# Halving the last RWKV norm, starting the output projection with the second half of the tokens, and moving the norms' low parts to VectorE

## The chip, the cores and the metric

The kernel runs on one core of one Trainium2 chip. The metric is the device time of one execution in microseconds, the median of several runs. A core has TensorE (PE, matmuls; weight loads are PEld), VectorE (DVE), ScalarE (ACT), GpSimd (POOL) and SyncE (SP, which issues most of the transfers). All five run their own instruction streams in order and wait for one another by semaphores. TensorE's clock has two levels, 1.2 and 2.4 GHz; a granted clock of 1.00 in the profile is the upper one, 0.50 the lower.

## What is computed

Two layers of a bidirectional encoder on 1024 tokens of width 1024, in float32. A layer is

```
h = rms_norm(x); proj = h @ w_in            # retention, RWKV-7, differential attention
y = concat(retention, rwkv7, attention)     # 8 blocks of 128 features: 0-2, 3-5, 6-7
x = x + y @ w_out                           # output projection
h = rms_norm(x); x = x + (silu(h @ w_gate) * (h @ w_up)) @ w_down
```

RWKV's result is normalised per head, gets a bonus, and is multiplied by a gate (`(norm(y) + bonus) * gate`) before it goes into `y`. Only that last step of RWKV (`rwkv_fin`), the projection with `w_out` and the RMS norms matter here.

## The kernel before

Activations lie with features on the 128 partitions and tokens in the free dimension. A tensor of 1024 x 1024 is 8 feature blocks k, each cut into two halves of 512 tokens; nearly every instruction works on a 128 x 512 tile. A dense product is made exact by splitting both factors into a high part and a low part (`split`: ACT writes the high part `hi`, then DVE or POOL subtracts it from the source to give `lo`), and by three matmuls hi*hi, hi*lo, lo*hi for each k (`dense`: 24 matmuls for 8 k). Tiles are called hh/hl (activations), sh/sl (activations of the Strassen-like sums) and whh/wll (weights); `wr` is a raw weight tile as loaded.

**The mixer's second part** (`rwkv`) interleaves, by a hand-written order on PE, ACT, DVE and POOL, the RWKV recurrence (`rwkv_rec`: one `U`, one `S` on ACT and a few small matmuls for every step, in windows w), the preparation of later windows, the retention (`ret_pair`, tile `rt` in its head norm) and, for each of three head pairs p, the last step `rwkv_fin`. In that order a list `beside` holds generators; every entry has a rate, and a `yield` is a place where other work is put in between. `rwkv_fin(p)` runs in the first window after pair p is complete, on both halves of the tokens at once; for the last pair it stands after everything else. Its head norm (`head_norm`, tile `fq`) is Square on ACT, a matmul `vps`, Ln on ACT, Exp on ACT, a product on DVE, a scale on ACT; Ln and Exp each load a function table. Then come the bonus (`bo`, loaded), the gate matmul `gps` (its operand `gl` is loaded), two DVE operations and a store to `mixed[3 + p]` in DRAM (`mix`). The recurrence runs through the tokens in both directions, so the second half of y is complete one window before the first half. Four buffers, a ring, are shared by y, bo, gl and the bonus's tiles; the later memory pools (H for hh/hl, W for weights) lie on the mixer's memory and a tile in them waits for the old tiles it overlaps.

**The output projection** (`phase_c`, `out_blocks`) loads the 16 half blocks of `mixed` (tile `mixl`, line 1421), first half first, splits them, loads all 16 tiles of x (line 1560), and then loads the w_out blocks (line 222). SP issues all of these, in the order in which a planner puts them out at compile time; the order follows the program text and modelled times. The first four output blocks cb are computed for half 0 and half 1 in turn, then cb 4 to 7 for half 0, then for half 1.

**The FFN's start** (`phase_c` after `out_blocks`) is the RMS norm of both halves (norm_sq, norm_rs with the matmul `nps` and the tile `nrs`, norm_out on line 262), and the operands of a Strassen-like scheme: B11, B21 from half 0, B22 from half 1, and the sums T1 to T4 (`ops_sums`), each with a split. About half of the low parts are made on POOL (`eng=gp` or `g`). The weights of the first gate and up blocks (q == 0) are split in 7 pieces each (`set_split`), low parts on POOL. `norm_split` at the start of a layer does the same with 16 tiles, low parts of odd k on POOL.

Of the kernel before, what the change touches and what calls it, by code (L numbers as in the profile page):

```python
# [17 lines left out]
T = 1024  # L18
# [159 lines left out]
class Net:  # L178
# [48 lines left out]

    def dense(self, ps, w, acts):

        n = len(acts)  # L230
        for k, (ah, al) in enumerate(acts):
            hi, lo = w[k]
            self.mm(ps, hi, ah, start=k == 0, stop=False)
            self.mm(ps, hi, al, start=False, stop=False)
            self.mm(ps, lo, ah, start=False, stop=k == n - 1)
# [572 lines left out]
    def head_norm(self, y, eps, w, b, q):  # L808

        nc = self.nc  # L810
        ps = []
        for half in range(2):
            self.act(q[:, half * 512:half * 512 + 512], y[half], AF.Square)
        yield 2
        for half in range(2):
            ps.append(self.bank([128, 512], "vps"))
            self.mm(ps[half], self.bones, q[:, half * 512:half * 512 + 512])
        yield
        for half in range(2):
            self.act(q[:, half * 512:half * 512 + 512], ps[half], AF.Ln, scale=1.0 / 64, bias=eps[:, 0:1])  # L820
            self.free(ps[half])
        self.act(q, q, AF.Exp, scale=-0.5)
        yield
        for half in range(2):
            sl = slice(half * 512, half * 512 + 512)
            self.tt(q[:, sl], y[half], q[:, sl], ALU.mult)
            self.act(q[:, sl], q[:, sl], AF.Identity, scale=w, bias=b)

    def rwkv_fin(self, l, st):
        nc = self.nc  # L830
        p = st["p"]
        pp = self.par[l][:, P_PAIR + p * PP:P_PAIR + (p + 1) * PP]
        yield
# [5 lines left out]
        for half in range(2):  # L839
            sl = slice(half * 512, half * 512 + 512)  # L840
# [5 lines left out]
        for half in range(2):  # L846
            sl = slice(half * 512, half * 512 + 512)
            t = q[:, sl]
            yield 1
            ps = self.bank([128, 512], "gps")  # L850
            self.mm(ps, lg, gl[half])
            self.tt(t, t, bo[half], ALU.add)
            yield
            self.tt(t, t, ps, ALU.mult)
            self.free(ps)
            nc.sync.dma_start(out=self.mixed[3 + p][:, sl], in_=t)

    def rwkv(self, l):
# [35 lines left out]
        for w in range(-2, 12):  # L894
# [57 lines left out]
        run(ret[0], self.rwkv_fin(l, sts[2]))  # L952
# [344 lines left out]
    def op(self, ops, name, t, eng=None):  # L1297
        p, tag = (self.S, "s") if name in ("T2", "T3", "T4") else (self.H, "h")
        ops[name].append(self.split(p, t, (tag, tag), eng=eng))

    def ops_sums(self, ops, bs, names=("T1", "T2", "T3", "T4")):

        g = self.nc.gpsimd
        for n in names:
            for i, (b11, b12, b21, b22) in enumerate(bs):
                e = g if i % 2 else None
                if n == "T1":
                    self.tt(b12, b12, b11, ALU.subtract)
                    self.op(ops, n, b12, g)
                elif n == "T2":  # L1310
                    self.tt(b22, b22, b12, ALU.subtract)
                    self.op(ops, n, b22, e)
                elif n == "T3":
                    self.tt(b11, b22, b11, ALU.subtract)
                    self.op(ops, n, b11, g)
                else:
                    self.tt(b21, b21, b22, ALU.subtract)
                    self.op(ops, n, b21, e)

    def set_load(self, src):  # L1320
# [7 lines left out]
        return dict(A11=a[:, :4], A12=a[:, 4:], A21=b[:, :4], A22=b[:, 4:], w={})  # L1328
# [38 lines left out]
    def out_blocks(self, l, x, acts):  # L1367

        order = [(cb, half) for cb in range(4) for half in range(2)]
        order += [(cb, half) for half in range(2) for cb in range(4, 8)]  # L1370
        w = {}
        for cb, half in order:
            if cb not in w:
                w[cb] = self.weights(self.ia["w_out"][l, cb])
            ps = self.psd.tile([128, 512], F32, tag="d", name="aps")
            self.dense(ps, w[cb], acts[half])
            self.tt(x[half][cb], ps, x[half][cb], ALU.add)
# [37 lines left out]
    def phase_c(self, l):  # L1415
        nc = self.nc
        acts = [[], []]
        for half in range(2):
            for k in range(8):
                m = self.S.tile([128, 512], F32, tag="s", name="mixl")  # L1420
                nc.sync.dma_start(out=m, in_=self.mixed[k][:, half * 512:half * 512 + 512])
                acts[half].append(self.split(self.H, m, ("h", "h")))
        x = self.load_x(self.xs)
        self.out_blocks(l, x, acts)
# [5 lines left out]
        gp = nc.gpsimd  # L1430
        with self.tc.high_priority(offset=100000):
# [6 lines left out]
            for k in range(8):  # L1438
                self.op(ops, "B21" if k >= 4 else "B11", self.norm_out(n[0], g, k, x[0], x[0][k]),
                        gp if k % 2 else None)  # L1440
            self.norm_sq(n[1], x[1], range(4, 8))
            self.norm_rs(n[1])
            for k in (4, 5, 6, 7, 0, 1, 2, 3):
                t = self.norm_out(n[1], g, k, x[1], x[1][k])
                if k >= 4:
                    self.op(ops, "B22", t, gp if k % 2 else None)
# [18 lines left out]
        return self.down(l, hid, xm)  # L1465
# [22 lines left out]
    def down(self, l, hid, xm):  # L1488
# [4 lines left out]
        for cb0 in (0, 4):  # L1493
            accs = []
            for half in range(2):
# [145 lines left out]
```

## Time and profile before

| | |
|---|---|
| time, median of 3 runs | 3538.19 us (3536.35 to 3542.45) |
| time of the profiled execution | 3539.07 us |
| its span, first to last instruction | 3537.3 us |
| PE busy | 3213.3 us (91%) |
| DVE, ACT, POOL busy | 2002.5, 1555.9, 941.8 us |
| mean granted TensorE clock | 0.951 |

The span is cut into stages. In layer 0 the mixer's second part ends near 940 us, the output projection runs from 976 to 1068 us, the FFN's first products from 1076 us on, and layer 1 begins near 1760 us; layer 1 repeats the pattern some 1747 us later. A busy time is read against its own stage: PE's 91% of the whole hides stretches in which it stands still.

### The profile page before, as it was taken

Reading aid. Unit: us, or ns where it says so; the run is one execution under the profiler, and the core shown is the slowest. Engines: PE = TensorE matmul, PEld = TensorE weight load, DVE = VectorE, ACT = ScalarE, POOL = GpSimd, SP = SyncE. Lnnn points to the kernel's source line nnn. Section 1 sums busy time; section 2 is a strip of 40 time slices with the busy share of each in tenths; the row PEclk is TensorE's granted clock in tenths of the full one; section 3 lists DMA queues with packets and bytes.
Section 4 is the critical chain, followed back from the end, with each engine's and each line's share of the span. In section 5 each row is a group of like instructions: output and inputs, shape, how many; then the busy total and the mean of one; then the engine's idle time right before and its main releaser. Section 6 shows DMA issues by size and latency. Waiting matters only on the chain.

```text
span 3537.3 us, 71264 instructions
## 1 busy us (share of the span) xinstructions
PE 3213.3 (91%) x29148; PEld 2595.5 (73%) x29148; DVE 2002.5 (57%) x3725; ACT 1555.9 (44%) x2975; POOL 941.8 (27%) x800
## 2 busy tenths in 40 slices
PE   6999799998697999999979997998986989999997
PEld 4778587777475888888867776877874768888886
DVE  4798526676338555552338975176662485555433
ACT  4566444656424333342236664356554333332322
POOL 3222220000036545422132221200001365544220
PEclk9999799999798999999999998999987999999998
DMA  5544324433431222283044533244425112223721
GB/s 172 153 144 121 116 104 156 137 118 107 144 105 60 84 75 92 78 286 119 27 159 129 153 110 124 98 155 141 138 75 188 72 51 93 78 78 117 264 72 48
DMA packets 214063, 419.02 MB, mean 118 GB/s; under 512 B 23876, under 2 KB 58948, under 8 KB 213700
## 3 DMA queue, kind: packets, MB, share of 16 engines
q1 hardware_dynamic: 191000, 378.53, 32.5%
q0 software_dynamic: 10064, 12.85, 1.7%
q10 hardware_dynamic: 12672, 23.07, 1.7%
q8 instruction: 230, 3.77, 0.5%
q14 instruction: 97, 0.79, 0.1%
HBM read 313.67 MB, written 100.70 MB: 117 GB/s over the span
## 4 chain that ended last, share of the span: by engine, by line
PE 72%; DVE 11%; DMA 6%; ACT 5%; issue 2%; POOL 2%; SPq 0%; DVEq 0%; ACTq 0%; POOLq 0%
PE sp L194 22%; PE dn L194 13%; PE dps L194 13%; PE aps L194 4%; DMA wr<-in_w_in_dram 2%; PE ns L194 2%; PE y L194 2%; DVE pt L1217 1%; PE pv L194 1%; PE tps L1247 1%; POOL wll L188 1%; ACT L185 1%; DVE x L188 1%; PE s L194 1%; PE yps L194 1%
## 5 line engine op out<-in xcount | busy, mean ns | idle before, releaser
L188 POOL TENSOR_TENSOR wll<-wr,whh 128x512 fp32r<-128x512 f32 x416 | 556.8, 1341 | 1576.6 <-ACT whh L185 1554.7
L185 ACT ACTIVATE whh<-wr 128x512 fp32r<-128x512 f32 x416 | 260.7, 630 | 627.2 <-PE sp L194 165.8
L194 PE MATMUL dps<-hl,whh 128*128 128x512 f32 x960 | 383.3, 399 | 6.7 <-POOL hl L188 3.5
L194 PE MATMUL dps<-hh,whh 128*128 128x512 f32 x960 | 386.9, 403 | 0.9 <-DVE stl L377 0.8
L194 PE MATMUL dps<-hh,wll 128*128 128x512 f32 x960 | 382.7, 399 | 1.2 <-POOL wll L188 1.2
L194 PE MATMUL sp<-hh,whh 128*128 128x512 f32 x704 | 278.2, 395 | 8.8 <-ACT hh L185 8.8
L194 PE MATMUL sp<-hl,whh 128*128 128x512 f32 x704 | 281.4, 400 | 2.8 <-POOL hl L188 2.5
L194 PE MATMUL sp<-hh,wll 128*128 128x512 f32 x704 | 276.4, 393 | 0.3 <-POOL wll L188 0.3
L194 PE MATMUL dn<-hh,whh 128*128 128x512 f32 x704 | 274.1, 389 | 2.4 <-ACT hh L185 2.4
L194 PE MATMUL dn<-hl,whh 128*128 128x512 f32 x704 | 274.9, 391 | 0.5 <-DVE hl L188 0.5
L194 PE MATMUL dn<-hh,wll 128*128 128x512 f32 x704 | 273.9, 389 | 0.0
L188 POOL TENSOR_TENSOR wll<-ws,whh 128x512 fp32r<-128x512 f32 x132 | 194.2, 1471 | 177.0 <-ACT whh L185 175.5
L188 DVE TENSOR_TENSOR hl<-hidr,hh 128x512 fp32r<-128x512 f32 x144 | 138.6, 979 | 171.2 <-ACT hh L185 163.1
L194 PEld LDWEIGHTS dps<-hl,whh 128*128 128x128 f32 x960 | 183.0, 191 | 52.4 <-POOL hl L188 6.1
L194 PE MATMUL sp<-sl,whh 128*128 128x512 f32 x528 | 212.9, 403 | 6.9 <-POOL sl L188 4.3
L194 PEld LDWEIGHTS dps<-hh,whh 128*128 128x128 f32 x960 | 183.4, 191 | 45.5 <-issue 4.4
L194 PE MATMUL sp<-sh,whh 128*128 128x512 f32 x528 | 211.8, 401 | 3.1 <-ACT as L185 3.1
L194 PE MATMUL sp<-sh,wll 128*128 128x512 f32 x528 | 213.3, 404 | 0.0
L194 PEld LDWEIGHTS dps<-hh,wll 128*128 128x128 f32 x960 | 182.7, 190 | 39.6 <-issue 2.4
L185 ACT ACTIVATE whh<-ws 128x512 fp32r<-128x512 f32 x132 | 83.3, 631 | 242.8 <-PE sp L194 138.7
L185 ACT ACTIVATE pt<-pt,mx 128x1024 f32<-128x1024 f32 x128 | 146.9, 1148 | 60.5 <-DVE mx L1221 58.3
L194 PEld LDWEIGHTS sp<-hh,whh 128*128 128x128 f32 x704 | 134.2, 191 | 40.0 <-ACT hh L185 9.7
(277 smaller groups left out, 7260.1 us busy)
## 6 DMA issues: line engine op xcount, KB each, us to landing
hidr<-hid SPq DMA_DIRECT2D x144, 256.0 KB, 5.1
bias<-t SPq DMA_DIRECT2D x64, 512.0 KB, 3.7
wr<-in_w_in_dram SPq DMA_DIRECT2D x120, 256.0 KB, 2.9
wr<-in_w_gate_dram SPq DMA_DIRECT2D x44, 512.0 KB, 3.6
wr<-in_w_up_dram SPq DMA_DIRECT2D x44, 512.0 KB, 3.4
wr<-in_w_down_dram SPq DMA_DIRECT2D x44, 512.0 KB, 4.0
pr<-st SPq DMA_DIRECT2D x56, 256.0 KB, 2.3
lo<-lod SPq DMA_DIRECT2D x48, 256.0 KB, 3.2
```

The lines of the kernel that those rows point to most:

```text
L185: self.nc.scalar.activation(out=out, in_=in_, func=func, **kw)
L188: (eng or self.nc.vector).tensor_tensor(out=out, in0=a, in1=b, op=op)
L194: self.nc.tensor.matmul(out, lhsT, rhs, start=start, stop=stop, **kw)
L1217: nc.vector.tensor_tensor_reduce(out=pt[:, sl], in0=ps, in1=bias[:, sl], scale=1.0, scalar=mx[:, 0:1] if kh else -3.0e38, op0=ALU.add, op1 ...
L1247: nc.tensor.transpose(ps[:, n * 128:(n + 1) * 128], P[0][:, c * 128:(c + 1) * 128], self.ident)
```

## The change

1. `rwkv_fin` takes a half: the second half runs in window j == 3 of its own pair, the first half in the next window (for the last pair: at the end). `head_norm` takes a list of tiles; here it gets one. Loads of bo and gl come ahead of the norm.
2. `phase_c` orders its work by use: second half of the tokens first; the blocks k in the order 6, 7, 0 to 5; the first two w_out blocks are loaded from POOL's queue; x is loaded block by block; four output blocks for the second half, then the same four for the first half, then cb 4 to 7 in the same way. From here to the end of the layer position 0 is the second half, and `down` works on position 1 first and returns the halves swapped back.
3. The low parts in `norm_split`, in the FFN's operands and sums, and of the first gate and up weights are made on DVE.

```diff
-    def weights(self, src):
+    def weights(self, src, queue=None):
...
-            nc.sync.dma_start(out=raw, in_=src[:, k0:k0 + step])
+            (queue or nc.sync).dma_start(out=raw, in_=src[:, k0:k0 + step])
...
-    def dense(self, ps, w, acts):
+    def dense(self, ps, w, acts, order=None):
...
-            h[half].append(self.split(self.H, t, ("h", "h"), eng=self.nc.gpsimd if k % 2 else None))
+            h[half].append(self.split(self.H, t, ("h", "h")))
...
-    def rwkv_fin(self, l, st):
+    def rwkv_fin(self, l, st, half):
...
-        q = self.Y.tile([128, T], F32, tag="fq", name="fq")
-        yield from self.head_norm(st["y"], self.eps64, pp[:, Q_LNW:Q_LNW + 1], pp[:, Q_LNB:Q_LNB + 1], q)
-        bo, gl = [], []
-        for half in range(2):
-            sl = slice(half * 512, half * 512 + 512)
-            bo.append(self.ring("bo"))
-            nc.sync.dma_start(out=bo[half], in_=self.bod[p][:, sl])
-            gl.append(self.ring("gl"))
-            nc.sync.dma_start(out=gl[half], in_=self.lod[2][:, sl])
+        bo = self.ring("bo")
+        nc.sync.dma_start(out=bo, in_=self.bod[p][:, sl])
+        gl = self.ring("gl")
+        nc.sync.dma_start(out=gl, in_=self.lod[2][:, sl])
+        q = self.Y.tile([128, 512], F32, tag="fq", name="fq", bufs=2)
+        yield
+        yield from self.head_norm([st["y"][half]], self.eps64, pp[:, Q_LNW:Q_LNW + 1], pp[:, Q_LNB:Q_LNB + 1], q)
...
+            if w >= 0 and j == 3:
+                beside.append([self.rwkv_fin(l, sts[p], 1), 10, 0, 0])
             if w > 0 and j == 0:
-                beside.append([self.rwkv_fin(l, sts[p - 1]), 13, 0, 0])
+                beside.append([self.rwkv_fin(l, sts[p - 1], 0), 10, 0, 0])
...
-        run(ret[0], self.rwkv_fin(l, sts[2]))
+        run(ret[0], self.rwkv_fin(l, sts[2], 0))
...
-        hi, lo = self.split(self.W, src, ("wh", "wl"), eng=self.nc.gpsimd)
+        hi, lo = self.split(self.W, src, ("wh", "wl"), eng=st["eng"])
...
+        ts = [slice(512, 1024), slice(0, 512)]
+        korder = (6, 7, 0, 1, 2, 3, 4, 5)
+        def load(half):
+            for k in korder:
+                m = self.S.tile([128, 512], F32, tag="s", name="mixl")
+                nc.sync.dma_start(out=m, in_=self.mixed[k][:, ts[half]])
+                acts[half][k] = self.split(self.H, m, ("h", "h"))
+        load(0)
+        for cb in range(2):
+            w[cb] = self.weights(self.ia["w_out"][l, cb], nc.gpsimd)
+        load(1)
+        for cb0 in (0, 4):
+            for half in range(2):
+                for cb in range(cb0, cb0 + 4):
+                    if cb not in w:
+                        w[cb] = self.weights(self.ia["w_out"][l, cb])
+                    t = x[half][cb] = self.ft("x")
+                    nc.sync.dma_start(out=t, in_=self.xs[cb][:, ts[half]])
+                    ps = self.psd.tile([128, 512], F32, tag="d", name="aps")
+                    self.dense(ps, w[cb], acts[half], korder)
+                    self.tt(t, ps, t, ALU.add)
...
-        return self.set_load([w[l, 2 * q], w[l, 2 * q + 1]])
+        return self.set_load([w[l, 2 * q], w[l, 2 * q + 1]], self.nc.gpsimd if q else None)
...
-                self.op(ops, "B21" if k >= 4 else "B11", self.norm_out(n[0], g, k, x[0], x[0][k]),
-                        gp if k % 2 else None)
+                self.op(ops, "B21" if k >= 4 else "B11", self.norm_out(n[0], g, k, x[0], x[0][k]))
...
-        return self.down(l, hid, xm)
+        x = self.down(l, hid, xm)
+        return x[::-1]
...
-            for half in range(2):
+            for half in (1, 0):
```

In `ops_sums` the engine arguments of the splits of T1 to T4 go in the same way.

## Rows read from the trace of the kernel before

**Rows 1.** Stages: us, busy by engine (count), granted clock, DMA share, GB/s.
```profile
550.00:930.00 380.00, 340.75 (x8588) 289.47 (x8586) 247.72 (x592) 213.57 (x537) 1.11 (x12) 0.93 0.38 123
930.00:980.00 50.00, 16.14 (x115) 9.40 (x115) 17.57 (x27) 28.12 (x45) 4.09 (x4) 0.59 0.71 243
...
1068.00:1125.00 57.00, 37.65 (x111) 25.02 (x110) 49.52 (x49) 25.21 (x40) 38.16 (x24) 0.76 0.11 37
...
1762.00:1800.00 38.00, 20.79 (x72) 13.55 (x72) 30.79 (x35) 21.27 (x34) 17.50 (x12) 0.82 0.23 80
...
2678.00:2728.00 50.00, 16.14 (x105) 9.26 (x100) 17.60 (x27) 27.61 (x44) 4.60 (x4) 0.59 0.72 247
```

**Rows 2.** Chain of waits from 820 to 1200 us: start, us, what.
```profile
939.98 0.44 DVE y L188
...
969.12 6.00 DMA wr<-in_w_out_dram
975.14 0.64 ACT whh L185
975.91 1.28 POOL wll L188
977.24 68.43 PE aps L194 x296
```

**Rows 3.** SP's issues in the same stretch: start, us, transfer, count.
```profile
937.17 3.86 SPq L1421 DMA_DIRECT2D mixl<-mix  x5
...
954.95 6.47 SPq L1421 DMA_DIRECT2D mixl<-mix  x10
961.77 6.99 SPq L1560 DMA_DIRECT2D x<-in_x_dram  x10
969.12 17.14 SPq L222 DMA_DIRECT2D wr<-in_w_out_dram  x8
```

**Rows 4.** ACT in order of time, last head norm and first splits.
```profile
943.23 0.69 ACT L185 ACTIVATE fq<-vps,eps 128x512 f32<-128x512 f32 x1 [0.34 <-PE vps L194]
944.94 0.69 ACT L185 ACTIVATE fq<-vps,eps 128x512 f32<-128x512 f32 x1 [1.02 <-PE vps L194]
945.64 1.28 ACT L185 ACT_TABLE_LOAD   x1
946.94 1.06 ACT L185 ACTIVATE fq<-fq 128x1024 f32<-128x1024 f32 x1
...
951.77 2.71 ACT L185 ACTIVATE hh<-mixl 128x512 fp32r<-128x512 f32 x5 [1.49 <-DVE fq L188]
```

**Rows 5.** DVE in order of time, the same stretch.
```profile
949.60 0.69 DVE L188 TENSOR_TENSOR fq<-fq,bo 128x512 f32<-128x512 f32 x1 [0.28 <-ACT fq L185]
...
951.00 0.68 DVE L188 TENSOR_TENSOR fq<-fq,bo 128x512 f32<-128x512 f32 x1
...
954.25 3.09 DVE L188 TENSOR_TENSOR hl<-mixl,hh 128x512 fp32r<-128x512 f32 x5
```

**Rows 6.** ACT's recurrence steps U: first, two around a head norm, last (96 steps).
```profile
571.19 0.21 ACT L185 ACTIVATE U<-x 128x64 f32<-128x64 f32 x1
...
846.24 0.22 ACT L185 ACTIVATE U<-x 128x64 f32<-128x64 f32 x1
...
860.99 0.21 ACT L185 ACTIVATE U<-x 128x64 f32<-128x64 f32 x1
...
938.75 0.22 ACT L185 ACTIVATE U<-x 128x64 f32<-128x64 f32 x1 [0.81 <-PE x L194]
```

**Rows 7.** Norm stretches by engine: FFN's start, then a half of layer 1's norm.
```profile
1051.30:1119.80 68.50, 49.33 (x170) 35.12 (x169) 60.84 (x56) 30.57 (x50) 46.91 (x29) 0.82 0.09 31
...
1786.30:1798.10 11.80, 9.57 (x35) 5.70 (x33) 11.77 (x12) 5.85 (x10) 6.32 (x4) 1.00 0.30 100
```

**Rows 8.** DVE's line 262 (norm_out) as the FFN's norm begins.
```profile
1051.37 2.08 DVE L262 SCALAR_TENSOR_TENSOR x<-x,par,nrs 128x512 f32<-128x512 f32 x3 [3.22 <-ACT nrs L185]
1053.36 0.69 DVE L188 TENSOR_TENSOR hl<-x,hh 128x512 fp32r<-128x512 f32 x1
```

More of the change, by code (lines that the diff above doesn't have):

```diff
@@ L226, in weights @@
         return w
-    def dense(self, ps, w, acts):
-        n = len(acts)
-        for k, (ah, al) in enumerate(acts):
+    def dense(self, ps, w, acts, order=None):
+        order = order or range(len(acts))
+        for k in order:
+            ah, al = acts[k]
             hi, lo = w[k]
-            self.mm(ps, hi, ah, start=k == 0, stop=False)
+            self.mm(ps, hi, ah, start=k == order[0], stop=False)
             self.mm(ps, hi, al, start=False, stop=False)
-            self.mm(ps, lo, ah, start=False, stop=k == n - 1)
+            self.mm(ps, lo, ah, start=False, stop=k == order[-1])
     def norm_sq(self, st, x, ks):
@@ L808, in head_norm @@
     def head_norm(self, y, eps, w, b, q):
-        nc = self.nc
+        n = len(y)
+        sl = [slice(i * 512, i * 512 + 512) for i in range(n)]
         ps = []
-        for half in range(2):
-            self.act(q[:, half * 512:half * 512 + 512], y[half], AF.Square)
-        yield 2
-        for half in range(2):
+        for i in range(n):
+            self.act(q[:, sl[i]], y[i], AF.Square)
+        yield n
+        for i in range(n):
             ps.append(self.bank([128, 512], "vps"))
-            self.mm(ps[half], self.bones, q[:, half * 512:half * 512 + 512])
+            self.mm(ps[i], self.bones, q[:, sl[i]])
         yield
-        for half in range(2):
-            self.act(q[:, half * 512:half * 512 + 512], ps[half], AF.Ln, scale=1.0 / 64, bias=eps[:, 0:1])
-            self.free(ps[half])
+        for i in range(n):
+            self.act(q[:, sl[i]], ps[i], AF.Ln, scale=1.0 / 64, bias=eps[:, 0:1])
+            self.free(ps[i])
         self.act(q, q, AF.Exp, scale=-0.5)
         yield
-        for half in range(2):
-            sl = slice(half * 512, half * 512 + 512)
-            self.tt(q[:, sl], y[half], q[:, sl], ALU.mult)
-            self.act(q[:, sl], q[:, sl], AF.Identity, scale=w, bias=b)
-    def rwkv_fin(self, l, st):
+        for i in range(n):
+            self.tt(q[:, sl[i]], y[i], q[:, sl[i]], ALU.mult)
+            self.act(q[:, sl[i]], q[:, sl[i]], AF.Identity, scale=w, bias=b)
+    def rwkv_fin(self, l, st, half):
         nc = self.nc
@@ L832, in rwkv_fin @@
         pp = self.par[l][:, P_PAIR + p * PP:P_PAIR + (p + 1) * PP]
+        sl = slice(half * 512, half * 512 + 512)
         yield
@@ L835, in rwkv_fin @@
         nc.sync.dma_start(out=lg, in_=self.ia["lora"][l, :, 1920 + p * 128:2048 + p * 128])
-        q = self.Y.tile([128, T], F32, tag="fq", name="fq")
-        yield from self.head_norm(st["y"], self.eps64, pp[:, Q_LNW:Q_LNW + 1], pp[:, Q_LNB:Q_LNB + 1], q)
-        bo, gl = [], []
-        for half in range(2):
-            sl = slice(half * 512, half * 512 + 512)
-            bo.append(self.ring("bo"))
-            nc.sync.dma_start(out=bo[half], in_=self.bod[p][:, sl])
-            gl.append(self.ring("gl"))
-            nc.sync.dma_start(out=gl[half], in_=self.lod[2][:, sl])
-        yield
[L846 to L856, printed above, removed]
+        bo = self.ring("bo")
[3 more added lines that the diff above has]
+        q = self.Y.tile([128, 512], F32, tag="fq", name="fq", bufs=2)
+        yield
+        yield from self.head_norm([st["y"][half]], self.eps64, pp[:, Q_LNW:Q_LNW + 1], pp[:, Q_LNB:Q_LNB + 1], q)
+        yield 1
+        ps = self.bank([128, 512], "gps")
+        self.mm(ps, lg, gl)
+        self.tt(q, q, bo, ALU.add)
+        yield
+        self.tt(q, q, ps, ALU.mult)
+        self.free(ps)
+        nc.sync.dma_start(out=self.mixed[3 + p][:, sl], in_=q)
     def rwkv(self, l):
@@ L1364, in ft, with out_blocks @@
         return self.F.tile([128, 512], F32, tag="f", name=name)
[L1367 to L1377, printed above, removed]
+    def out_blocks(self, l):
+        nc = self.nc
+        ts = [slice(512, 1024), slice(0, 512)]
+        acts, x, w = [[None] * 8, [None] * 8], [[None] * 8, [None] * 8], {}
+        korder = (6, 7, 0, 1, 2, 3, 4, 5)
[18 more added lines that the diff above has]
+                    self.tt(t, ps, t, ALU.add)
+        return x
     def ffn_set(self, l, name, q):
         w = self.ia[name]
-        return self.set_load([w[l, 2 * q], w[l, 2 * q + 1]])
+        return self.set_load([w[l, 2 * q], w[l, 2 * q + 1]], self.nc.gpsimd if q else None)
     def ffn_first(self, st, ops):
@@ L1416, in phase_c @@
         nc = self.nc
[L1417 to L1424, printed above, removed]
+        x = self.out_blocks(l)
         xm = [self.dr.tile([128, T], F32, name=f"xm{l}_{k}") for k in range(8)]
@@ L1429, in phase_c @@
         n = [dict(pool=(self.S, "s")) for _ in range(2)]
-        gp = nc.gpsimd
         with self.tc.high_priority(offset=100000):
@@ L1494, in down @@
             accs = []
-            for half in range(2):
+            for half in (1, 0):
                 for cb in range(cb0, cb0 + 4):
```

22 lines of the change are left out of this document (10 added, 12 removed).

## The prediction

> **What bounds the kernel now.** I began with the busy time by stages. The reader is to see three kinds of stretch [rows 1]: the mixer's second part (550 to 930 us), where PE is busy 341 of 380 us; the passage into the output projection (930 to 980 us), where PE is busy 16 of 50 us at a mean clock of 0.59; and the norms, at 1068 to 1125 us 38 of 57 us with DVE busy 50 and POOL 38, and at 1762 to 1800 us 21 of 38 us. Layer 1 repeats the first passage to the digit: 16.14 us of PE in 50 [rows 1].
>
> Next, the chain of waits through the passage [rows 2]. The recurrence's last sum is made at 939.98, but the unbroken run of projection matmuls starts only at 977.24, and what ends the wait is no arithmetic of the mixer: a 6.00 us transfer of w_out, then its split on ACT and POOL. SP's issues say why [rows 3]: ten mixl, ten x and then the weights stand in one queue, so the first weights were issued at 969.12. ACT's order of time gives the head norm and its end [rows 4]: the first hh split starts at 951.77 although its tile had been loaded from 937 us on [rows 3], and the releaser named is DVE's fq. That is the second bonus sum at 951.00 [rows 5]: the split's buffer lies on memory which that sum still reads.
>
> Last, the norms by engine and by instruction [rows 7, 8]. In the FFN's start DVE is busy 60.8 of 68.5 us with 56 instructions, 1.09 us each; in the same time POOL runs 29. Alone, the same kinds of instruction start 0.60 us apart (five hl, (3.09 - 0.69)/4 [rows 5]) or 0.66 us apart (three norm_out, (1053.36 - 1051.37)/3 [rows 8]). So DVE pays for every POOL split beside it, and POOL takes its own time from DVE; the two hardly run in parallel here.
>
> **The change part by part**, against the profiled execution's 3539.07 us (its span is 3537.3; the median of the runs is 0.9 lower). Prices are for a layer unless said.
>
> *The last norm's first half, and the start of the projection.* With one half the chain from the last sum loses the second vps and Ln (944.94 - 943.23 = 1.71) and half of Exp (0.53) [rows 4]. The first half's bonus sum, at 949.60 now [rows 5], moves to 947.4. But pair 2's second half is now normalised during the recurrence's last steps, on the same ACT: two table loads (2 x 1.28), Ln 0.69, half of Exp 0.53 [rows 4], and Square and scale at about Ln's price, together 5.2. I take 5; bounds are 0 (it fills ACT's waits) and 7.0, what a whole norm costs the recurrence (below). The bonus sum so ends the norm at 952.4, and the first hh starts 0.77 later as now (951.00 to 951.77), at 953.1: I keep the wait on old memory, since the pools stay where they are. Eight hh at 2.71/5 = 0.54 take 4.3 [rows 4]; from the first whh to the unbroken run are 2.1 us (975.14 to 977.24 [rows 2]). Start: 959.5 instead of 977.24, **17.7 gained**. Its bounds are 8 (the queues, below) and 28 (no wait on memory). The weights are off the path then: on POOL's queue nothing is ahead of them, and POOL is idle; if POOL issues late, the eight hh cover 4 us. The second half's first four blocks are 96 matmuls, 22.2 us at the chain's 296 in 68.43 [rows 2]: the first half's store, load and split, behind each other on SP, have that long. Swapping halves in xm, hid and down moves no work: cost nothing, covered by PE.
>
> *The norms by halves in the two earlier pairs.* A whole norm costs the recurrence: the two steps around one last 860.99 - 846.24 = 14.75 us, while the mean step is (938.75 - 571.19)/95 = 3.87 [rows 6], so 7.0 more. Two halves repeat the two table loads: 2.6 us of ACT per pair. Bounds: 0 if ACT's waits on PE hide them, 7.0 if a half costs as much as a whole. I take 2.6, since Ln, Exp, Square and scale stay the same in sum: **5.2 lost** for two pairs.
>
> The Trainium skill (ScalarE: Activation LUTs, "What ACT_TABLE_LOAD costs") adds some 1.38 us of drain to each load. The trace does not show it: Exp starts at 946.94, 0.02 after its load's end [rows 4]. By that page three more norms a layer, each with two loads, would cost 8.3 more a layer, and the sum would be some 17 us later.
>
> *The FFN's start.* All 29 POOL low parts of that stretch go to DVE: 85 instructions, 16 of them norm_out, 16 x 0.66 + 69 x 0.60 = 52.0, and the 7.7 us in which DVE waited for the norm's sum stay [rows 7]. 59.7 instead of 68.5: **8.8 gained**. Bounds: 2 (every instruction at its full 0.69: 85 x 0.69 + 7.7 = 66.4) and 16 (the waits are filled as well). POOL's cover goes: ACT's high parts remain beside DVE, at 30.6 of 68.5 us. What comes late next is T4, then the elementwise work of gate and up, where POOL's splits for the next weights still contend.
>
> *norm_split at a layer's start.* A half now takes 11.77 us for 12 DVE instructions with 4 on POOL [rows 7]; all 16 on DVE are 8 x 0.66 + 8 x 0.60 = 10.1, so 1.7 less. In the other half DVE also empties PSUM or makes sums; I count **1.7 gained** for both halves (bounds 0 and 3.4).
>
> Sum: 17.7 - 5.2 + 8.8 + 1.7 = 23.0 a layer, 46 for two: 3539.1 - 46 = 3493.1, or 3492 against the median.
>
> **The rivals.**
> A. *DVE becomes the bound and stays at the contended price* (slower). If POOL moves the next blocks' weight splits into the freed time, DVE goes on paying 1.09 us each: 85 x 1.086 + 7.7 = 100.0, 31.5 lost; and in norm_split 16 x 0.98 = 15.7 instead of 11.8 in each half, 7.8 lost. With 17.7 - 5.2 gained that is 26.8 lost a layer: 3592. It decides from 0.83 us an instruction, where 117 of them eat the 12.5 gained. For it: DVE is without a pause in these stretches already. Against: the next weights need buffers that the first ones hold, and without POOL the trace shows 0.60.
> B. *Every half norm costs the recurrence as much as a whole one* [rows 6]: 14.0 lost in the two earlier pairs, and the start 2 later. 15.7 - 14.0 + 8.8 + 1.7 = 12.2 a layer: 3514. For it: latency between ACT, PE and DVE does not shrink with the tile.
> C. *The splits do not wait for the ring.* The second half's loads are issued by 941 [rows 3] and land as a w_out block does, 6.00 later [rows 2]; run at 949.1, 28.1 gained, 33.4 a layer: 3471. For it: only the first of the hh buffers needs to be the one on old memory. Against: the five hh stood in line behind it [rows 4].
> D. *The order of use isn't what the queues give*: all 16 mixl and the first two weight blocks, 5 MB, move ahead of the first product. Ten mixl, ten x and one weight block, 5.5 MB, took from 954.95 to 975.1 [rows 2, 3]; 5 MB take 18.4, from 946 to 964.4, run at 966.5, 10.7 gained, 16.0 a layer: 3506. The change would then not do what it says.
> The Trainium skill (DMA: Bandwidth & Descriptors, "Issuing engines are not separate DMA queues") speaks for D: transfers started by another engine share the same 16 DMA engines, and only issue time is saved. Here the place in SP's line is what cost (8 us of issues between 961.77 and 969.12), which that rule leaves open.
>
> **How the numbers follow.** Forecast 0.50, C 0.20, B 0.12, D 0.10, A 0.08. The likeliest is 3492; its own bounds are about 3470 to 3510. The range 3455 to 3525 takes in C, D and B with some room and leaves A out. A measurement of this kernel can tell about 0.2%, 7 us: faster than that 0.88 (all but A and the edge of B and D), within it 0.04, slower 0.08.
>
> **What would show it.** Right: the projection's run starts 25 us or less after the recurrence's last sum (now 37), w_out's first loads stand ahead of x; DVE in the FFN's start near 0.62 us each with POOL all but idle; in the earlier windows, two norms for each pair with four table loads. Wrong: hh splits before the bonus sum (C), steps around a half norm at 7 us above the mean (B), a first product that waits for weights or the second half's mixl (D), DVE above 0.83 us an instruction (A).

## The result and the profile after

The changed kernel takes 3483.53 us (median of 4 runs, 3480.39 to 3490.52), the kernel before beside it 3538.26 us (4 runs): a ratio of 0.9846, 95% interval 0.9828 to 0.9865, or 54.7 us faster. Forecast were 46 us less, 3492, in a range of 3455 to 3525. The profiled execution of the changed kernel is the longest of its four, 3490.52 us, which is 48.6 us below the profiled one of the kernel before.

Busy time by stages of the changed kernel, with the columns of [rows 1, 7]:

```profile
930.00:980.00 50.00, 31.00 (x214) 21.18 (x211) 26.27 (x32) 34.36 (x56) 14.26 (x10) 0.76 0.63 219
1039.70:1092.30 52.60, 43.18 (x169) 31.83 (x168) 50.70 (x83) 30.86 (x51) 0.00 (x0) 0.94 0.11 41
```

The reader is to see two stretches in which PE stands still less. In the passage into the projection PE is busy 31.00 of 50 us (16.14 before) and its mean clock is 0.76 (0.59) [rows 1]. The FFN's start, from the first norm_out to the end of T4, takes 52.6 us instead of 68.5 [rows 7]: DVE does 83 instructions in 50.70 us, 0.61 each, where it did 56 in 60.84, and POOL does nothing in it.

The chain of waits of the changed kernel, from the recurrence's end to the FFN's second norm (start, us, what), answers to [rows 2]:

```profile
948.94 0.93 PE y L194 x12
950.35 0.63 ACT fq L185
951.00 1.28 ACT L185
952.29 0.69 ACT fq L185
953.00 1.28 ACT L185
954.29 0.64 ACT fq L185
...
958.40 4.29 DMA mixl<-mix
962.73 1.72 POOL wll L188
964.49 67.85 PE aps L194 x286
...
1060.65 1.28 ACT L185
1061.94 0.69 ACT nrs L185
1062.65 1.28 ACT L185
1063.94 0.64 ACT nrs L185
1064.61 2.08 DVE x L263 x3
```

The recurrence's last sum now starts at 949.89 and the unbroken run of projection matmuls at 964.49: 14.6 us, before 37.3 [rows 2]. No transfer of w_out is in the chain any more. What is left is the head norm, with its two table loads of 1.28 us, the splits that follow it on ACT (six hh from 957.25 on, the first whh at 960.39), and the low parts of the weights on POOL. The load of mixl that the chain names ahead of the last low part landed at 962.69, while POOL was still at the low part before, which had waited for that whh (below). But the last sum itself comes later, 949.89 instead of 939.98, although the recurrence began within 0.8 us of its old place: 571.97 [rows 6: 571.19].

SP's issues in this stretch, against [rows 3]:

```profile
948.08 5.30 SPq L1376 DMA_DIRECT2D mixl<-mix  x8
958.04 0.32 SPq L853 DMA_DIRECT2D mix<-fq  x1
958.40 4.25 SPq L1376 DMA_DIRECT2D mixl<-mix  x8
963.45 0.99 SPq L1389 DMA_DIRECT2D x<-in_x_dram  x2
964.82 0.33 SPq L222 DMA_DIRECT2D wr<-in_w_out_dram  x1
```

and POOL's:

```profile
950.91 1.18 POOL L222 DMA_DIRECT2D wr<-in_w_out_dram  x2 [140.90 <-DMA gl<-lod]
961.14 6.67 POOL L188 TENSOR_TENSOR wll<-wr,whh 128x512 fp32r<-128x512 f32 x4 [9.04 <-ACT whh L185]
```

The first two w_out blocks are issued 1.0 us after the last sum and ahead of all of x; before it was 29.1 us, behind ten tiles of x.

### The profile page after: what moved, and what is told of

It is laid out like the page before. It is cut to its first block, busy times and chain, and to the rows that moved or that the text cites. A ratio compares the mean times of both kernels' runs of the same rounds, so it can differ in the third digit from the quotient of the medians.

```text
span 3488.7 us, 71259 instructions
## 1 busy us (share of the span) xinstructions
PE 3209.4 (92%) x29148; PEld 2596.5 (74%) x29148; DVE 1994.8 (57%) x3805; ACT 1568.5 (45%) x2993; POOL 824.5 (24%) x724
## 4 chain that ended last, share of the span: by engine, by line
PE 75%; DVE 11%; ACT 7%; DMA 3%; issue 2%; POOL 1%; SPq 0%; DVEq 0%; ACTq 0%; POOLq 0%
PE sp L194 22%; PE dps L194 14%; PE dn L194 13%; PE aps L194 5%; PE ns L194 2%; ACT L185 2%; PE y L194 2%; DMA wr<-in_w_in_dram 1%; PE pv L194 1%; PE tps L1247 1%; DVE pt L1217 1%; PE s L194 1%; PE btp L194 1%; PE pps L194 1%; PE yps L194 1%
## 5 line engine op out<-in xcount | busy, mean ns | idle before, releaser
L188 POOL TENSOR_TENSOR wll<-wr,whh 128x512 fp32r<-128x512 f32 x400 | 541.4, 1356 | 1452.7 <-ACT whh L185 1262.0
L188 POOL TENSOR_TENSOR wll<-ws,whh 128x512 fp32r<-128x512 f32 x120 | 175.6, 1463 | 175.2 <-ACT whh L185 169.1
L194 PEld LDWEIGHTS dn<-hh,whh 128*128 128x128 f32 x704 | 133.2, 189 | 33.3 <-ACT hh L185 5.4
```

The lines of the kernel that those rows point to most:

```text
L188: (eng or self.nc.vector).tensor_tensor(out=out, in0=a, in1=b, op=op)
L194: self.nc.tensor.matmul(out, lhsT, rhs, start=start, stop=stop, **kw)
```

## The experiments

Four stages hold the differences. The table gives, for layer 0 and layer 1 of each profiled execution, in us: from the recurrence's first U to its last sum; from there to the first projection matmul; from there to the first store of hid; and from the first to the last matmul of down. The median is of the runs timed. e9 is one run of e3's program without any change, for a second profile; its label says more than that.

| kernel | U to last sum | sum to projection | projection to hid | down | median |
|---|---|---|---|---|---|
| before | 368.8, 367.9 | 35.9, 36.0 | 159.1, 159.2 | 240.9, 240.9 | 3538.3 |
| changed | 377.9, 374.6 | 12.2, 13.5 | 146.1, 144.8 | 243.4, 244.7 | 3483.5 |
| e1, before + part 3 | 368.1, 366.1 | 35.8, 34.8 | 144.0, 144.0 | 240.9, 240.9 | 3501.1 |
| e2, without part 3 | 374.6, 373.6 | 12.3, 13.1 | 164.0, 163.9 | 244.9, 244.4 | 3525.2 |
| e3, early norms whole | 373.7, 372.0 | 12.9, 13.0 | 145.5, 145.0 | 244.9, 245.0 | 3479.0 |
| e4, hh off the ring | 374.3, 372.0 | 15.9, 15.6 | 145.5, 145.3 | 243.8, 243.8 | 3485.4 |
| e5, hid in order of use | 377.4, 374.9 | 13.1, 13.5 | 145.8, 144.8 | 240.9, 240.9 | 3474.6 |
| e6, x ahead of w_out | 377.3, 377.3 | 31.1, 31.9 | 144.8, 144.8 | 243.5, 244.6 | 3521.2 |
| e7, as e4, other place | 374.4, 376.0 | 13.4, 14.2 | 145.1, 144.7 | 243.6, 244.9 | 3482.7 |
| e8, all norms whole | 368.3, 362.6 | 16.6, 16.5 | 150.2, 148.8 | 243.8, 243.8 | 3483.3 |
| e9, as e3 | 370.9, 373.8 | 12.5, 13.3 | 144.3, 145.4 | 243.7, 243.6 | 3477.9 |
| e10, norm_split on POOL | 371.9, 374.0 | 13.1, 13.1 | 145.3, 145.8 | 243.6, 243.6 | 3487.5 |
| e11, first weights on POOL | 374.7, 378.3 | 13.2, 12.7 | 156.1, 156.2 | 243.8, 243.8 | 3503.7 |
| e12, e3 + e5 | 370.7, 371.6 | 12.2, 13.3 | 146.1, 144.9 | 240.9, 242.6 | 3475.3 |

The first column spreads by some 6 us between kernels that treat the norms alike. Part of that is no difference of the programs: e3 and e9 are one program, and differ in it by 2.8 and 1.8 us. So it is read by its means.

### Part 3 alone, and all but part 3 (e1, e2)

e1 is the kernel before with the changed `norm_split`, `op`, `ops_sums` and `set_split`; e2 is the changed kernel with the old ones (two places of e2's edit):

```diff
-        ops[name].append(self.split(p, t, (tag, tag)))
+        ops[name].append(self.split(p, t, (tag, tag), eng=eng))
...
-        return self.set_load([w[l, 2 * q], w[l, 2 * q + 1]], self.nc.gpsimd if q else None)
+        return self.set_load([w[l, 2 * q], w[l, 2 * q + 1]], self.nc.gpsimd)
...
```

> The kernel before with part 3 of the change alone (all low parts of norm_split, of the FFN's operands and sums and of the first gate and up weights on DVE). Theory (POOL beside DVE is what costs): the stretch from the projection's run to the first hid store, 157.6 us in layer 0 and 159.2 in layer 1 of the kernel before, becomes 144 to 149, the whole 3510 to 3520 us; DVE near 0.62 us an instruction. Rival (the order of the halves carries a third or more of that stretch's gain): 149 to 153 and 3520 to 3530. Rival A of the prediction (DVE keeps the contended price): over 3560. For the start of a layer the theory expects no gain: up to the first attention score product 3 us earlier, and nothing of it left at the first U.

> The changed kernel without part 3 (low parts back on POOL as in the kernel before). Theory (the price on DVE): 3502 to 3512 us, run to first hid 154 to 158 us instead of 143.7, the projection's run still 14 to 16 us after the last sum. Rival (the order of the halves made the FFN's start shorter): 3490 to 3500 and 147 to 152 us.

e1: 3501.09 us, ratio 0.9896 (0.9883 to 0.991), 37.6 us faster than before by part 3 alone. e2: 3525.2 us, 0.9967 (0.9954 to 0.9979): the other two parts alone give 13.5 us. Each is outside what the theory expected (3510 to 3520 and 3502 to 3512), on the side on which part 3 is worth more, and neither is near its rival: the stretch up to hid is 144.0 us in e1, and in e2 it is 164.0, 4.9 longer than before, which nothing here explains. Part 3 is worth 37.6 us put in first and 41.7 put in last (3525.2 - 3483.5), so some seven tenths of the gain are the engine of the low parts. The same FFN stretch, from the first norm_out to the end of T4, by engine in e1:

```profile
1049.50:1101.80 52.30, 43.66 (x166) 30.82 (x165) 50.08 (x82) 30.31 (x49) 0.00 (x0) 0.96 0.12 41
```

and in e2:

```profile
1036.40:1108.10 71.70, 49.48 (x174) 34.04 (x173) 62.86 (x56) 31.40 (x51) 47.46 (x30) 0.85 0.09 30
```

Where e1's DVE takes 0.61 us for one instruction, e2's takes 1.12. At 0.61 its 56 would need 34.2 us, so 28.7 us of DVE's time went to POOL's 30 splits: 0.96 us for each. DVE's instructions come in two lengths there: 29 of the 56 take 0.7 to 0.8 us, as without POOL, and 26 take 1.7 to 1.8. A low part made on POOL so cost DVE more than making it itself.

### Which of POOL's splits (e11)

```diff
-        return self.set_load([w[l, 2 * q], w[l, 2 * q + 1]], self.nc.gpsimd if q else None)
+        return self.set_load([w[l, 2 * q], w[l, 2 * q + 1]], self.nc.gpsimd)
```

> The changed kernel with the low parts of the first gate and up weights (14 a layer) back on POOL; operands and sums of the FFN stay on DVE. Theory (any POOL split beside DVE makes DVE's instructions slower by 0.5 to 1 us while it runs; 14 of POOL's 29 come back, and 14 fall off DVE's list, 8.4 us): projection's first matmul to first hid store 148 to 154 us instead of 144.8 to 146.1, the whole 3488 to 3500. Rival 1 (only the low parts of operands and sums matter): 144 to 147 us and 3481 to 3486. Rival 2 (the first weights carry it all): 162 us or more.

3503.69 us, 0.9906 (0.989 to 0.9923), 20 us slower than the changed kernel; projection to hid 156.1 us. That is 10.7 us a layer for 14 splits, 2 us beyond the theory's stretch of 148 to 154, and both rivals fall. The FFN stretch by engine, then DVE's two rows with which a norm's wait ends, in e11:

```profile
1035.50:1100.30 64.80, 46.90 (x169) 34.03 (x168) 57.11 (x74) 31.68 (x51) 18.52 (x12) 0.86 0.10 33
```

```profile
1062.11 0.69 DVE L188 TENSOR_TENSOR nsq<-nsq 128x512 f32<-128x512 f32 x1 [0.69 <-ACT nsq L185]
1068.40 4.16 DVE L263 SCALAR_TENSOR_TENSOR x<-x,par,nrs 128x512 f32<-128x512 f32 x3 [5.59 <-ACT nrs L185]
```

The second norm's wait in the kernel before, then the same in the changed kernel, to be set beside [rows 8]:

```profile
1082.36 4.16 DVE L262 SCALAR_TENSOR_TENSOR x<-x,par,nrs 128x512 f32<-128x512 f32 x3 [5.59 <-ACT nrs L185]
...
1064.61 2.08 DVE L263 SCALAR_TENSOR_TENSOR x<-x,par,nrs 128x512 f32<-128x512 f32 x3 [1.75 <-ACT nrs L185]
1066.60 0.68 DVE L188 TENSOR_TENSOR hl<-x,hh 128x512 fp32r<-128x512 f32 x1
1067.20 0.74 DVE L263 SCALAR_TENSOR_TENSOR x<-x,par,nrs 128x512 f32<-128x512 f32 x1
```

Two things return with the 12 splits in this window. DVE pays (57.11 - 74 x 0.61)/12 = 1.0 us for each. And its wait for the second norm is 5.59 us again, as before, not 1.75. The wait has two parts. In the changed kernel DVE still has 2.4 us of work after the norm's last sum (two low parts of weights, 1060.37, and two sums of weights, up to 1062.87), where in e11 and before it has none. And the chain from that sum to `nrs` is 1.45 us shorter, most of it in the two matmuls `nps`, in the kernel before and in the changed kernel:

```profile
1076.82 2.07 PE L194 MATMUL nps<-nsq,ones 128*128 128x512 f32 x2 [8.33 <-DVE nsq L188]
1060.51 1.12 PE L194 MATMUL nps<-nsq,ones 128*128 128x512 f32 x2 [2.39 <-DVE nsq L188]
```

Before, PE had begun the FFN's products at 1066.06 (not only from 1076 us on), then stood still for 8.33 us, and its granted clock over these two matmuls was 0.50, the lower level; in the changed kernel it had stood still for 2.39 us, and the clock was 1.00. In e11 they take 2.08 us after 9.62.

### The price of the halves (e3, e9, e8)

e3 gives pairs 0 and 1 the old whole `rwkv_fin` (here `rwkv_fin2`); e8 gives it to all three:

```diff
-            if w >= 0 and j == 3:
+            if w == 11:
                 beside.append([self.rwkv_fin(l, sts[p], 1), 10, 0, 0])
             if w > 0 and j == 0:
-                beside.append([self.rwkv_fin(l, sts[p - 1], 0), 10, 0, 0])
+                beside.append([self.rwkv_fin2(l, sts[p - 1]), 13, 0, 0])
...
```

> The changed kernel with the norms of the two earlier pairs whole again, only the last pair by halves. Theory (more table loads in the recurrence cost, 2.6 us for each of two pairs a layer): U to last sum 372 to 375 us instead of 377.9 (368.8 before), the whole 3473 to 3479. Rival (ACT's waits hide the earlier pairs' loads, the loss is that of the last pair's second half): 377 us, the whole 3481 to 3486. Rival B (a half costs what a whole norm does): 364 to 370 us, 3463 to 3471.

> The kernel of e3 once more, for a second profile of the same program. Theory (a half norm in the earlier pairs costs the recurrence 1 to 2 us each): U to last sum 372 to 374 us again in layer 0 and 371 to 373 in layer 1. Rival (e3's 373.7 and 372.0 lie within the spread of the kernels with six halves, 372.0 to 377.9): 375 us or more in one of the layers.

> The changed kernel with all norms whole, parts 2 and 3 as they are. Theory (the halves are a draw: what the last pair's half adds to the recurrence is what the shorter end gives): U to last sum 368 to 370 us, first projection matmul 19 to 22 us after it, so U to that matmul 387 to 392 against 388 to 390 in the changed kernel; the whole 3479 to 3488. Rival 1 (the halves pay): 24 us or more after the sum, 3490 or more. Rival 2 (the halves cost, as the prediction's terms for the recurrence say): first matmul 15 us after the sum, 3470 to 3477.

e3: 3479.01 us, 0.9829 (0.9816 to 0.9843), not to be told from the changed kernel's 0.9846. e8: 3483.31 us, 0.9845 (0.9829 to 0.986), the changed kernel's time to 0.2 us: the halves are a draw, as the theory said. Its stages are not: the first projection matmul comes 16.6 us after the last sum, not 19 to 22, and U to that matmul is 384.9 and 379.1 us, not 387 to 392. The first column tells what each costs the recurrence. Eight kernels with six halves have a mean of 375.2 us (16 values, 371.9 to 378.3); e3, e9 and e12 with whole early norms 372.1 (6 values, 370.7 to 373.8); the three kernels with whole norms 367.0 (6 values, 362.6 to 368.8). The two earlier pairs' halves so cost some 3.1 us a layer, the last pair's 5.1. e9's 370.9 and 373.8 met neither the theory nor its rival cleanly, and the first two means differ by about as much as the values of one kernel do, so the 3.1 is a rough size.

What e8 wins in the recurrence it loses behind it. Its chain of waits:

```profile
952.62 0.70 DVE fq L188
953.33 5.27 DMA mix<-fq
958.62 0.33 SPq L1406
...
962.90 7.19 DMA wr<-in_w_out_dram
970.12 0.64 ACT whh L185
...
973.83 26.20 PE aps L194 x107
```

PE waits again after its first projection matmuls, since one store of the last norm holds up SP's line: the loads of `mixl` behind it wait 5.27 us for it to land, and the next w_out blocks stand behind those. The run is unbroken only 35 us after the sum; up to there PE stands still for 4.0 us in all, as much as the stretch to hid is longer than the changed kernel's (150.2 and 146.1). The changed kernel has the second half's store out of the way by then.

### The place of the weights in the line (e6)

```diff
         load(0)
-        for cb in range(2):
-            w[cb] = self.weights(self.ia["w_out"][l, cb], nc.gpsimd)
         load(1)
+        x = self.load_x(self.xs)[::-1]
...
```

> The changed kernel with all 16 tiles of x loaded ahead of the first w_out block on SP, as in the kernel before (halves, k order and everything else as in the change). Theory (the place of the weights in SP's line sets the projection's start, norm by halves or not): weights issued some 24 us after the last sum, first projection matmul 29 to 33 us after it instead of 12.2 to 13.5, the whole 3514 to 3525. Rival (the halves alone brought most of the earlier start): 18 to 22 us and 3495 to 3503.

3521.16 us, 0.9955 (0.9941 to 0.9968): 37.6 us slower than the changed kernel, and the first projection matmul 31.1 and 31.9 us after the last sum, as the theory had it. SP's issues and ACT's first weight split in e6:

```profile
954.72 3.77 SPq L1376 DMA_DIRECT2D mixl<-mix  x8
958.54 11.20 SPq L1566 DMA_DIRECT2D x<-in_x_dram  x16
970.08 12.12 SPq L222 DMA_DIRECT2D wr<-in_w_out_dram  x6
```

```profile
976.11 5.01 ACT L185 ACTIVATE whh<-wr 128x512 fp32r<-128x512 f32 x8 [11.41 <-DMA wr<-in_w_out_dram]
```

ACT has split all the activations by then and waits 11.41 us for weights which SP issued 24 us after the sum, behind 11.20 us of x. The halves alone leave the start nearly where it was (35.9 before). The edit takes the weights off POOL's queue and puts them behind x in one step; which of the two counts more is not told apart.

### The split that waits for the ring (e4, e7)

e4 puts a tile of its own on the old memory; e7 does the same with the zeroing behind the first weights:

```diff
+        z = self.H.tile([128, 512], F32R, tag="h", name="hz")
+        nc.gpsimd.memset(z.bitcast(F32), 0.0)
         load(0)
```

> The changed kernel with one more tile in the pool of hh and hl, allocated first and set to zero on POOL, so that it and not the first hh takes the buffer that lies on the ring. Theory (the split waits for the ring, but ACT is in the last head norm until 955.7 anyway): first hh 1 to 1.5 us earlier, the projection's run 13 to 14 us after the last sum instead of 14.6, the whole 3480 to 3483. Rival C of the prediction (without that wait the splits run ahead of the last head norm): run 8 to 10 us after the last sum, 3470 to 3476. No change at all would say that the wait was never the limit.

> As e4, but the zeroing stands behind the issue of the first weights on POOL, so that they are no longer held up by it. Theory (e4 lost 3 us because its zeroing waited for the ring ahead of the weights on POOL's queue; the splits themselves ran earlier): hh from 6.5 us after the last sum, first projection matmul 10.5 to 12 us after it (12.2 and 13.5 in the changed kernel, 15.9 and 15.6 in e4), the whole 3479 to 3483. Rival (the weights are late for another reason): 15 to 16 us again.

e4: 3485.37 us, 0.9853 (0.9839 to 0.9866), no faster, and the projection starts 15.9 us after the sum. ACT and POOL in e4, whose last sum starts at 943.32:

```profile
949.11 0.81 ACT L185 ACTIVATE fq<-fq,par 128x512 f32<-128x512 f32 x1 [0.76 <-DVE fq L188]
949.83 3.73 ACT L185 ACTIVATE hh<-mixl 128x512 fp32r<-128x512 f32 x7
957.49 0.63 ACT L185 ACTIVATE whh<-wr 128x512 fp32r<-128x512 f32 x1 [3.92 <-DMA wr<-in_w_out_dram]
```

```profile
950.84 0.53 POOL L1380 MEMSET hz<- 128x512 f32 x1 [145.45 <-DMA mixl<-mix]
951.35 1.18 POOL L222 DMA_DIRECT2D wr<-in_w_out_dram  x2
```

The same rows of ACT in the changed kernel, last sum at 949.89:

```profile
955.68 0.81 ACT L185 ACTIVATE fq<-fq,par 128x512 f32<-128x512 f32 x1 [0.76 <-DVE fq L188]
957.25 1.15 ACT L185 ACTIVATE hh<-mixl 128x512 fp32r<-128x512 f32 x2 [0.76 <-DVE fq L188]
```

Without the ring's wait the first hh follows the head norm's last step at once, 6.5 us after the sum instead of 7.4. That is all there was to win, 0.85 us: ACT executes in order, and the head norm stands ahead of the splits. But now the zeroing waits on POOL. It starts at 950.84, just after the bonus sum, which ends at 950.65, has let go of the ring; the load of mixl that its row names landed in the same 0.1 us. The weights behind it go out 8.0 us after the sum instead of 1.0, so that ACT waits 3.92 us for them. This shows, by accident, that POOL's queue helps only while nothing waits in it. e7 (3482.69 us, 0.9843, 0.983 to 0.9857) did not do what it was for: its first hh has the wait of 0.76 us on DVE again, so with the later zeroing the first hh was again the tile that waited for the ring; its first projection matmul (13.4 and 14.2 us after the sum) met neither the theory nor the rival. What an unheld start without late weights would give was not measured; by e4 it is under 1 us a layer.

### The order in which down loads (e5, e12)

```diff
-        r = []
-        for half in range(2):
+        r = [None, None]
+        for half in (1, 0):
             t = self.ft("hidr")
             self.nc.sync.dma_start(out=t, in_=hid[f][:, half * 512:half * 512 + 512])
-            r.append(self.split(self.H, t, ("h", "h")))
+            r[half] = self.split(self.H, t, ("h", "h"))
```

> The changed kernel, in which the down product loads and splits the two halves of each hidden block in the order in which it multiplies them (position 1 first). Theory (the change turned the order of the multiplication round but not that of the loads, so the first products wait for the tile that is loaded second): first down matmul 391.3 us after the first hid store instead of 392.3 and 392.9, first to last down matmul 240.9 us as in the kernel before instead of 243.4 and 244.7, the whole 7 to 10 us below the changed kernel's 3483.5: 3474 to 3477. Rival (these microseconds are chance in when transfers land): stretches of 243 to 245 again and 3481 to 3487.

3474.58 us, 0.9811 (0.9796 to 0.9826), some 9 us below the changed kernel, whose interval it does not touch; down takes 240.9 us again. PE's only waits at down's beginning, in the kernel before:

```profile
1525.92 0.49 PE L194 MATMUL dn<-hh,whh 128*128 128x512 f32 x1 [0.87 <-ACT hh L185]
1526.64 0.50 PE L194 MATMUL dn<-hl,whh 128*128 128x512 f32 x1 [0.23 <-DVE hl L188]
```

in the changed kernel:

```profile
1500.48 0.50 PE L194 MATMUL dn<-hh,whh 128*128 128x512 f32 x1 [1.93 <-ACT hh L185]
1502.03 0.50 PE L194 MATMUL dn<-hl,whh 128*128 128x512 f32 x1 [1.05 <-DVE hl L188]
```

and in e5:

```profile
1497.68 0.50 PE L194 MATMUL dn<-hh,whh 128*128 128x512 f32 x1 [1.19 <-ACT hh L185]
1498.40 0.50 PE L194 MATMUL dn<-hl,whh 128*128 128x512 f32 x1 [0.23 <-DVE hl L188]
```

The change made `down` multiply position 1 first, while `hid_split` still loaded and split position 0 first. The first products so wait for the tile that is ready second. The waits are only part of the loss. Against e5 the two are together 1.6 us longer in layer 0 and 3.5 in layer 1, while the stretch from hid's first store to down's last matmul is 3.2 and 6.0 longer. Behind the waits the granted clock falls to the lower level, in layer 0 for some 3.5 us, and that is where the rest goes; in e5 it does not fall (the changed kernel, then e5):

```profile
1502.60:1506.00 3.40, 3.40 (x10) 2.64 (x9) 3.40 (x5) 1.53 (x4) 1.28 (x1) 0.52 0.93 328
1499.00:1503.00 4.00, 4.00 (x19) 3.32 (x18) 4.00 (x5) 2.38 (x5) 1.79 (x2) 1.00 0.98 313
```

The changed kernel's 10 matmuls in 3.4 us stand beside e5's 19 in 4.0.

> e3 and e5 together: the changed kernel with the two earlier pairs' norms whole and with the hidden blocks loaded in the order in which down multiplies them. Theory (the two savings lie in different stages and add): first to last down matmul 240.9 us in both layers, U to last sum 372 to 374 us, the whole 3467 to 3472, below every kernel so far. Rival (e3's 4 us are spread and only e5's order counts): 3473 to 3476.

e12: 3475.29 us, 0.9817 (0.9803 to 0.983), the same as e5: by the time the rival held. `down` takes 240.9 us in layer 0, but 242.6 in layer 1, where the granted clock is at the lower level for some 3 us after the first products, although the wait between them is as short as in e5 (0.23 us). e5 and e12, not to be told apart, are the best that was found, and beat both kernels.

### norm_split alone (e10)

The old `norm_split`, low parts of odd k on POOL, in the changed kernel:

```diff
-            h[half].append(self.split(self.H, t, ("h", "h")))
+            h[half].append(self.split(self.H, t, ("h", "h"), eng=self.nc.gpsimd if k % 2 else None))
```

> The changed kernel with norm_split alone back on POOL for odd k. Theory (the split at a layer's start ends 3 us earlier on DVE, but the next stage, paced by its weights and by DVE's own work, takes most of it back): 1 to 2 us a layer, the whole 3485 to 3488 against 3483.5. Rival (nothing is left of it): 3481 to 3485. The prediction's term is 1.7 us a layer.

3487.48 us, 0.9856 (0.9838 to 0.9874): 4 us more for two layers, but the interval overlaps the changed kernel's. The traces say more. The first U of layer 0 comes at 572.0 us on average in the three kernels with that split on POOL (before, e2, e10: 571.2 to 572.6) and at 570.4 in the other eleven (568.9 to 572.0). From down's last matmul in layer 0 to the first U of layer 1 the means are 553.7 (552.7 to 555.0) and 549.8 (548.3 to 552.7). So by the means the gain is 1.6 us in layer 0, where the two groups overlap, and 3.9 in layer 1: within and above the theory's 1 to 2, while the time alone does not show it. What e1 expected (nothing left at the first U) does not fit the means; its own first U came at 569.8, inside the spread. The profiled execution of the changed kernel is the one with both highest values, 572.0 and 552.7, and hides the gain.

## Why the prediction was right, by its own steps

The time and the direction came out as forecast, and so did the signs to look for: a start 14.6 us after the last sum, w_out ahead of x, DVE at 0.61 us with POOL idle, and 16 table loads instead of 10 between the first U and the last sum of layer 0. Of the terms two were as sized and three were not.

That the sum came so near is in part luck. Forecast were 25 us for parts 1 and 2 in two layers, 2 x (17.7 - 5.2), and 21 for part 3, 2 x (8.8 + 1.7). Measured are 13.5 (e2) to 17.1 (54.7 - 37.6, by e1) and 37.6 to 41.7: part 3 brought about twice its share, parts 1 and 2 some six tenths of theirs, and what they lack is mostly the 9 us that `down` lost (e5).

- *Start of the projection, 17.7 gained.* From the last sum to the unbroken run 22.7 us are won (37.3 to 14.6); the last pair's half in the recurrence costs 5.1 (forecast 5). Net 17.6. The order of the chain is as written (bonus sum, hh, whh, run), but its pieces are not, and their errors cancel: first hh 7.4 us after the last sum (8.1 forecast), first whh 3.1 later (4.3), the run 4.1 after that (2.1). The last piece is longer because the run waits for two low parts on POOL, of 1.6 and 1.7 us. What carries the gain is the place of the weights in the queues: with them behind x again 18.9 of the 22.7 us are gone (e6). The step had that as its condition ("off the path then").
- *Two earlier pairs by halves, 5.2 lost.* About 3.1, by means that spread as much; where the rest went is not shown. The upper bound was misread: of the two steps whose 14.75 us gave "7.0 more" for a whole norm, the first holds 6.02 us of ACT's waiting for y up to 852.47, ahead of the norm's first instruction at 853.02. In the changed kernel the same step, without a norm in it, takes 5.7 us (856.57 to 862.26); the second step, with the norm's Ln, is 6.74, 2.9 above the mean.
- *The FFN's start, 8.8 gained.* Mis-sized: 15.9 us (68.5 to 52.6). The price for each instruction was right, 50.70/83 = 0.61. What failed is "the 7.7 us in which DVE waited for the norm's sum stay". They shrank to 1.9 us: in the second norm's wait DVE now has work, and with PE standing still less the norm's two matmuls ran at the upper clock. Both go when the weights' splits go back to POOL (e11). The time came out at the upper bound of 16, "the waits are filled as well".
- *norm_split, 1.7 gained.* Some 1.6 us in layer 0 and 3.9 in layer 1 by the means above, 2.0 a layer by e10's time: 2.8 on average, inside the bounds of 0 and 3.4, layer 1 above them.
- *Swapping halves in xm, hid and down: nothing.* Wrong, and the only step with the wrong sign: some 4.5 us a layer are lost (e5). The step said that no work moves and PE covers it. The order of use in `down` had been turned, the order of the loads that feed it had not; at the stage's first products PE stood still for 1.93 and 1.05 us instead of 0.87 and 0.23, and its clock then fell to the lower level for 3.5 us.

Summed by these readings, with a minus for a gain: -17.6 + 3.1 - 13.9 (projection run to first hid, 157.6 to 143.7, of the 15.9) - 2.8 + 4.5 = -26.7 a layer, 53 for two; measured are 54.7 by the medians, 48.6 between the two profiled executions.

Of the rivals, A (DVE stays at the contended price) had the right mechanism at the wrong place: e2 and e11 are that price, and no POOL split was left in the stretch to set it. The Trainium skill (SBUF — State Buffer, "Who interferes with whom") says that a DVE instruction with two SBUF inputs contends with a GpSimd instruction that reads SBUF. The runs agree: a split that takes POOL 1.28 us where DVE stands still (975.91 [rows 2]) took 0.96 us from DVE in e2. B (a half costs a whole norm, 14.0) did not come: 3.1, and the four steps with a half norm's Ln in the recurrence's earlier pairs are 5.7 to 8.1 us long in layer 0, 1.7 to 4.2 above the mean of 3.97, not 7. C (no wait for the ring) is excluded: the first hh starts as the bonus sum ends, and e4, which took that wait away, won 0.85 us in front of the splits. D (the queues turn the order of use round) did not come: the run starts 14.6 us after the last sum, and the second eight mixl are issued from 958.40 on, behind the weights (950.91). e6 is not D, since x and not mixl stands ahead there, but shows the size of a late place: 37.6 us. The Trainium skill (DMA: Bandwidth & Descriptors, "Issuing engines are not separate DMA queues") says that starting transfers on several engines saves only the time it takes to initiate them, usually small beside the transfer. Here that time is not small: SP issues 16 tiles of x for 11.20 us in e6, and ten of them for 6.99 us before [rows 3] (not the 8 of the prediction).

What stays open: how much of e3's 4.5 us is real, why projection to hid is 1 to 2 us longer in the changed kernel than in e1, and why parts 1 and 2 make that stretch 4.8 us longer where POOL keeps its splits (e2).

## What to carry to other kernels

Read an engine's price for one instruction with and without its neighbour before sharing work between the two: here a split handed to POOL took 1.0 us from DVE, where DVE does it in 0.61. When an order of use is turned round, follow it back through every load and split that feeds it, and look at the first product of the stage: there a tile that came second held PE up, and the lower clock behind the wait cost nearly as much again. And in a queue that issues in order, ask what each load stands behind: moving two w_out blocks past x and the last store was worth more than shortening the arithmetic ahead of them.

## What was not expected of the hardware

- Work moved onto the busier engine shortened that engine's own wait: DVE's 5.59 us for the second norm became 1.75 with 27 instructions more in the stretch. 2.4 us of it were filled; the rest is a shorter chain, mostly two matmuls of 1.12 us instead of 2.07, at a granted clock of 1.00 instead of 0.50.
- The mean granted clock of the FFN's start rose from 0.82 [rows 7] to 0.94, though PE's work there is the same; PE only stood still less, 9.4 us of 52.6 instead of 19.2 of 68.5.
- Two waits of 1.93 and 1.05 us at the start of `down` were followed by 3.4 us at a granted clock of 0.52; two of 1.19 and 0.23 us in e5 by none. Between them it is not settled: 1.50 and 0.23 us in e12's layer 1 were followed by 3 us at 0.50, 1.55 and 0.23 us in layer 1 of the kernel before by none.
- A split on POOL either leaves a DVE instruction at 0.7 us or stretches it to 1.7 to 1.8; little lies between (e2).
- A transfer issued from POOL waits like any other instruction in its line: in e4 a zeroing of 0.53 us, held up until the ring was free, put off the weights behind it by 7 us.
